# The sums of a recurrence with the heads' halves exchanged, and its value products moved into a second job

## The chip, the cores and the metric

The kernel runs on one core of a Trainium2 chip. The metric is the time of one execution on the device in microseconds (us). Three executions of the kernel before took 1149.68 to 1152.16 us, with a median of 1150.76.

## The reference

One layer of a diffusion backbone is computed for 128 context tokens and 512 latent tokens, 640 in all. It has two branches, a recurrence in both directions (RWKV-7, 8 heads of 64) and a neighbourhood attention, whose outputs are gated, merged and followed by a feed-forward part. The change lies in the recurrence:

```python
def _wkv_step(s, inp):
    r, w, k, v, a, b = inp
    sa = jnp.einsum("bhvk,bhk->bhv", s, a)
    s = s * w[:, :, None, :] + sa[..., None] * b[:, :, None, :] + v[..., None] * k[:, :, None, :]
    return s, jnp.einsum("bhvk,bhk->bhv", s, r)
...
    s_f, y_f = _wkv_scan(s0[:, 0], rh, ..., False)
    s_b, y_b = _wkv_scan(s0[:, 1], rh, ..., True)
    y = y_f + y_b
    mean = jnp.mean(y, axis=-1, keepdims=True)
    var = jnp.mean(jnp.square(y - mean), axis=-1, keepdims=True)
```

Each head carries a state s of 64x64 from token to token. Every token reads the state with r, and the outputs of the two directions are summed to y and normalised per head.

## The kernel before, in words

The recurrence is not run token by token. The 640 tokens form 10 blocks of 64 ("slots": 0 to 7 latent, 8 and 9 context), and with two directions each pair of heads has 20 "lines", one for each block and direction. Within a line everything is a product of 64x64 matrices; between the lines of a sequence runs the state. The four pairs of heads (ct 0 to 3) are worked through one after the other. The two heads of a pair lie on the partitions 0 to 63 and 64 to 127 (`hrows[0]`, `hrows[1]`), so that a product of 64x64 uses one quarter of TensorE's array: which rows of the array says where its input lies, which columns says where its output goes. A product with `hrows[h]` for both is on a diagonal quarter, one that goes from `hrows[h]` to `hrows[1 - h]` on the other two.

For each pair there are four stages:

- `main` makes the matrices N of all lines (`n_job`).
- `inv` inverts a triangular matrix for each line in 30 steps on VectorE (DVE). At three of the steps, named by a table, it lets TensorE (PE) do a group of lines: first lines 8 to 11, then 0 to 7, then 12 to 19. For a group, `v_job` turns v by products with an identity (`idh(h)`) and copies it to ZV on ScalarE (ACT); `t_job` turns B and K and copies them to TG; `g_job` makes the products that are masked on DVE to AG and TG. The value products of lines 10 to 19 (`flip`) already stand in `g_job`. At the end the inverse is put together as Rt (L1345 to L1364).
- `carry`, the sweep, takes the eight steps s in turn, with two lines each (four in steps 0 and 1, where the context blocks go along). A step has three phases. In the first, PE makes AG·ZV (L1400), which ACT copies to x0 (L1403); then PE adds the outputs of the step before to Y (`ysum`, L1380), begins the new state `pn` by products of the identity with ZV (L1415), and adds R·ZV to Y (L1421). In the second, PE multiplies Rt with x0 (L1430) and ACT copies the result to ZV (L1436). In the third, PE finishes `pn` (L1443) and DVE scales it to the ZV of the next line (L1455). Between the phases the generator yields, and a plan written out by hand puts in a number of matmuls of a projection that does not depend on the recurrence ("fillers", L223). Y is two accumulators, one for the slots 0 to 7, copied to y at the sweep's end (L1462), and one for the slots 8 and 9, copied at step 2 (L1406).
- `out` normalises y with statistics from matmuls (L1472) and passes it on.

The accumulators (`wps()`) are taken in turn from six buffers. On every engine the instructions stand in the order in which the program issues them.

The identity products and the Y products, as they stand before:

```python
                    for g, (sl, d, l) in todo:
                        for h in range(2):
                            if sl != 8:
                                own = hrows[h]
                                pe.matmul(pn[own, g * 64:g * 64 + 64], idh(h), ZV[own, l, h, :],
                                          start=once(pn, h), stop=False)
```

Of the kernel before, what the change touches and what calls it, by code (L numbers as in the profile page):

```python
# [108 lines left out]
def V(ap, dims, off=0):  # L109

    return bass.AP(ap.tensor, ap.offset + off, [list(ap.ap[0])] + [list(d) for d in dims])
# [3 lines left out]
def body(ctx: ExitStack, tc: tile.TileContext, xs, xp, cols, consts, w_ada, b_row, w_rw, w_qkv,  # L115
# [3 lines left out]
    pe, act, dve, pool, sp = nc.tensor, nc.scalar, nc.vector, nc.gpsimd, nc.sync  # L119
# [40 lines left out]
    def idh(h):  # L160
        return K[64 * h:64 * h + 64, KO["ident"] + 64 * h:KO["ident"] + 64 * h + 64]
# [935 lines left out]
    with ExitStack() as s3:  # L1097
# [12 lines left out]
        v = vp0  # L1110
# [10 lines left out]
        def wps():  # L1121
            return pp.tile([P, 512], F32, tag="w", bufs=6, name=nm("w"))
# [53 lines left out]
        def sq(t, n):  # L1176
            return V(t[:, :], [[64, n], [1, 64]])
# [18 lines left out]
        def g_job(S, l0, l1):  # L1196
            n = l1 - l0

            f0 = max(l0, 10)
            pv = wps() if l1 > f0 else None  # L1200
            pg, pr = wps(), (wps(), wps())
            for l in range(l0, l1):
                if l >= f0:
                    flip(pv, l, f0)
                o_ = slice(64 * (l - l0), 64 * (l - l0) + 64)
                b, k = (S.BK[l // 10][:, l % 10, i, :] for i in range(2))
                for h in range(2):
                    pe.matmul(pg[hrows[1 - h], o_], k[hrows[h], :], AG[hrows[h], l, h, :], start=True, stop=True)
                for x, i in ((b, 0), (k, 1)):
                    for h in range(2):  # L1210
                        pe.matmul(pr[h][hrows[h ^ i], o_], x[hrows[h], :], R_[hrows[h], l, :],
                                  start=True, stop=True)
            ls = slice(l0, l1)
            if l1 > f0:
                v_out(pv, f0, l1 - f0)

            def masks():
                for h in range(2):
                    oth = hrows[1 - h]
                    dve.tensor_tensor(out=AG[oth, ls, h, :], in0=sq(pg, n)[oth],  # L1220
                                      in1=V(K[oth, :], [[0, n], [1, 64]], KO["strict"]), op=ALU.mult)
                for h in range(2):
                    dve.tensor_tensor(out=TG[:, ls, h, 1, :], in0=sq(pr[h], n),
                                      in1=V(K[:, :], [[0, n], [1, 64]], KO["incl"]), op=ALU.mult)

            return masks

        def v_job(S, l0, l1):

            if l0 > 9:  # L1230
                return
            n = min(l1, 10) - l0
            pv = wps()
            for l in range(l0, l0 + n):
                for h in range(2):
                    pe.matmul(pv[hrows[1 - h], 64 * (l - l0):64 * (l - l0) + 64], v[hrows[h], 64 * l:64 * l + 64],
                              idh(h), start=True, stop=True)
            v_out(pv, l0, n)

        def v_out(pv, l0, n):  # L1240
            for h in range(2):
                act.copy(ZV[hrows[1 - h], l0:l0 + n, h, :], sq(pv, n)[hrows[1 - h]])

        def flip(pv, l, l0):

# [122 lines left out]
        def carry(ct, S, last):  # L1368
# [4 lines left out]
            Y = [wps(), wps()]  # L1373
            begun, back = [], []

            def ysum(items):

                for (sl, d, l) in items:
                    for h in range(2):
                        pe.matmul(V(Y[sl // 8][hrows[h], :], *ycol(sl, d)), ZV[:, l, h, :], TG[:, l, h, 1, :],  # L1380
                                  start=once(Y[sl // 8], h), stop=sl in (7, 9) and d == 1)

            def once(t, h):
# [4 lines left out]
            def ycol(sl, d):  # L1388

                n = 8 if sl < 8 else 2  # L1390
                return ([[-1, 64]], 64 * (n - sl % 8) - 1) if d else ([[1, 64]], 64 * (sl % 8))

            for s in range(8):
# [9 lines left out]
                act.copy(x0[:, :ng, :], V(px[:, :], [[64, ng], [1, 64]]))  # L1403
                ysum(back)
                if s == 2:
                    act.copy(y[:, 512:640], Y[1][:, 0:128])  # L1406
                todo = [(g, i) for g, i in enumerate(items) if i[0] != 7]
                if todo:

                    pn = wps()  # L1410
                    for g, (sl, d, l) in todo:
                        for h in range(2):
                            if sl != 8:
                                own = hrows[h]
                                pe.matmul(pn[own, g * 64:g * 64 + 64], idh(h), ZV[own, l, h, :],  # L1415
                                          start=once(pn, h), stop=False)
                for (sl, d, l) in items:
                    for h in range(2):
                        own = hrows[h]
                        if sl != 8:  # L1420
                            pe.matmul(V(Y[sl // 8][own, :], *ycol(sl, d)), ZV[own, l, h, :], R_[own, l, :],  # L1421
                                      start=once(Y[sl // 8], h), stop=False)
                if s == 7 and not PRM["lh"][ct]:
                    last()
                yield
# [33 lines left out]
                if s == 7:  # L1459
                    ysum(items)  # L1460
                yield
            act.copy(y[:, 0:512], Y[0][:, 0:512])  # L1462

        def out(ct, S):

# [694 lines left out]
```

## Time and profile before

| | before |
|---|---|
| median of three runs | 1150.76 us (1149.68 to 1152.16) |
| the profiled execution | 1150.25 us |
| its span in the trace | 1148.5 us |
| PE matmul busy | 1115.5 us, 97% of the span |
| PE weight loads busy | 989.1 us, 86% |
| DVE busy | 778.9 us, 68% |
| ACT busy | 535.4 us, 47% |
| GpSimd (POOL) busy | 195.3 us, 17% |
| recurrence in the span | from about 256 to 629 us |

The span is what the trace covers, and 1.75 us of the profiled execution lie around it. Busy times of PE are those of its matmuls, whose ends are modelled; the loads of weights (PEld) run beside them. A float32 product of 64x64 stands in the trace as two records. In a row of the trace, "out<-in" names the tiles, "128x64" the partitions and elements, "x8" the records grouped, and the bracket tells how long the engine had been idle and which instruction it had waited for.

### The profile page before, as it was taken

What the parts mean: (1) busy time and instruction counts of PE and PEld (TensorE: products, weight loads), DVE (VectorE), ACT (ScalarE), POOL (GpSimd) and SP (SyncE); (2) the same over time, 40 slices, a digit from 0 to 9 for tenths busy, and PEclk for the clock granted to TensorE, in tenths of its full rate; (3) what the DMA queues carried; (4) which work ended last, traced back from release to release, by engine and by line L of the source; (5) the groups of instructions that cost most, each with busy time, mean ns of one, the idle gap of its engine ahead of it and who ended that gap; (6) DMA issues with size and microseconds to landing.
All of it is one profiled execution on the core that took longest, in us unless ns stands there. A gap on an engine that the chain in (4) does not pass through costs nothing.

```text
span 1148.5 us, 26859 instructions
## 1 busy us (share of the span) xinstructions
PE 1115.5 (97%) x11160; PEld 989.1 (86%) x11160; DVE 778.9 (68%) x1641; ACT 535.4 (47%) x1052; POOL 195.3 (17%) x262
## 2 busy tenths in 40 slices
PE   6999999999999999999999999999999999999998
PEld 4688878789888988888898788999899989998997
DVE  4565465769558847945786846897478747874775
ACT  4444566655465665556343525654134413441340
POOL 1163244320101202120100521110101010101000
PEclk9999999999999999999999999999999999999999
DMA  9752677654433533343733971223212321232122
GB/s 341 264 119 83 205 277 230 203 150 122 109 75 86 142 91 93 107 108 86 268 108 105 269 213 67 92 93 94 90 56 92 95 90 55 92 96 89 55 92 93
DMA packets 60482, 149.16 MB, mean 130 GB/s; under 512 B 7460, under 2 KB 22436, under 8 KB 60360
## 3 DMA queue, kind: packets, MB, share of 16 engines
q1 hardware_dynamic: 54888, 131.16, 34.8%
q0 software_dynamic: 4032, 14.68, 6.5%
q8 instruction: 88, 1.44, 0.5%
q10 hardware_dynamic: 1440, 1.59, 0.5%
q14 instruction: 34, 0.28, 0.1%
HBM read 118.41 MB, written 14.32 MB: 116 GB/s over the span
## 4 chain that ended last, share of the span: by engine, by line
PE 74%; DVE 10%; issue 8%; ACT 3%; DMA 3%; POOL 1%; SPq 0%; DVEq 0%; ACTq 0%; POOLq 0%
PE acc L311 24%; PE f L1863 21%; PE fl L223 9%; PE mm L223 5%; DVE RL L1321 1%; DVE pr L1317 1%; PE lg L959 1%; PE po L1006 1%; PE pt L988 1%; PE psa L1044 1%; DVE Rt L1353 1%; DMA wa<-in_w_ada_dram 1%; DMA f<-in_w_ada_dram 1%; PE w L1400 1%; PE w L1430 1%
## 5 line engine op out<-in xcount | busy, mean ns | idle before, releaser
L1863 PE MATMUL f<-t,whi 128*128 128x320 f32 x640 | 141.7, 309 | 0.2
L311 PE MATMUL acc<-whi,u 128*128 128x512 f32 (+1 forms) x448 | 136.0, 385 | 0.0
L1863 PE MATMUL f<-b,whi 128*128 128x320 f32 x608 | 135.0, 310 | 0.4 <-DVE b L212 0.4
L223 PE MATMUL fl<-h,whi 128*128 128x320 f32 x672 | 120.8, 320 | 0.0
L1863 PEld LDWEIGHTS f<-t,whi 128*128 128x128 f32 x640 | 106.8, 188 | 0.8 <-issue 0.4
L223 PEld LDWEIGHTS fl<-h,whi 128*128 128x128 f32 x672 | 101.1, 188 | 4.8
L192 ACT CAST whi<-wst 128x1024 fp32r<-128x1024 f32 (+1 forms) x77 | 79.4, 1034 | 54.5 <-PE acc L311 41.8
L1863 PEld LDWEIGHTS f<-b,whi 128*128 128x128 f32 x608 | 101.7, 188 | 1.1 <-issue 0.6
L1863 PE MATMUL f<-t,wlo 128*128 128x320 f32 x320 | 98.9, 309 | 0.0
L311 PEld LDWEIGHTS acc<-whi,u 128*128 128x128 f32 x448 | 83.5, 188 | 16.7
L1863 PE MATMUL f<-b,wlo 128*128 128x320 f32 x304 | 94.0, 309 | 0.0
L1916 ACT CAST whi<-ws 128x1024 fp32r<-128x1024 f32 x40 | 42.1, 1053 | 104.4 <-PE f L1863 45.6
L311 PE MATMUL acc<-wlo,u 128*128 128x512 f32 (+1 forms) x224 | 86.3, 385 | 0.0
L1930 POOL TENSOR_TENSOR ws<-wst 128x512 f32<-128x512 f32 x20 | 29.0, 1449 | 334.9 <-DVE wlo L1919 226.3
L195 DVE TENSOR_TENSOR wlo<-wst,whi 128x1024 fp32r<-128x1024 f32 (+2 forms) x57 | 60.9, 1077 | 30.7 <-ACT whi L192 30.0
L311 PE MATMUL acc<-whi,h 128*128 128x512 f32 x240 | 78.9, 403 | 0.7 <-DVE h L436 0.7
L1731 DVE SCALAR_TENSOR_TENSOR tt<-acc,G 128x512 f32<-128x512 f32 (+1 forms) x51 | 34.7, 680 | 59.3 <-PE acc L311 45.4
L223 PE MATMUL fl<-h,wlo 128*128 128x320 f32 x336 | 63.0, 318 | 0.0
L1916 ACT CAST whi<-wst 128x1024 fp32r<-128x1024 f32 (+1 forms) x48 | 41.4, 870 | 42.3 <-PE acc L311 25.1
L1863 PEld LDWEIGHTS f<-t,wlo 128*128 128x128 f32 x320 | 60.1, 188 | 0.0
L1919 DVE TENSOR_TENSOR wlo<-ws,whi 128x1024 fp32r<-128x1024 f32 x40 | 55.5, 1387 | 5.4 <-ACT whi L1916 5.4
L1455 DVE TENSOR_TENSOR ZV<-w,Dt 64x128 f32<-64x128 f32 x64 | 18.5, 289 | 58.7 <-PE w L1443 57.6
(342 smaller groups left out, 2536.3 us busy)
## 6 DMA issues: line engine op xcount, KB each, us to landing
wst<-in_w_dram SPq DMA_DIRECT2D x66, 512.0 KB
wst<-in_w_rw_dram SPq DMA_DIRECT2D x31, 512.0 KB
wlo<-wst POOLq DMA_DIRECT2D x28, 512.0 KB, 4.9
wa<-in_w_ada_dram SPq DMA_DIRECT2D x24, 512.0 KB
f<-in_w_ada_dram SPq DMA_DIRECT2D x16, 512.0 KB
wst<-in_w_qkv_dram SPq DMA_DIRECT2D x12, 512.0 KB
o<-o_d SPq DMA_DIRECT2D x14, 320.0 KB
x<-in_xs_dram SPq DMA_DIRECT2D x8, 512.0 KB
```

Of the source, the lines that this page charges most:

```text
L192: act.copy(hi[:, :n], st[:, :n])
L195: dve.tensor_tensor(out=lo[:, a:b], in0=st[:, a:b], in1=hi[:, a:b].bitcast(F32), op=ALU.subtract)
L223: pe.matmul(ps[:, :t1 - t0], w[:, a:a + 128], x[:, k0 + kt, t0:t1], start=n == 0, stop=n == 3 * nk - 1)
L311: pe.matmul(pss[i][:, a:b], lhs(x, kt, ts_), w[:, cs_], start=ki == 0 and n == 0, stop=ki == last and n == 2)
L959: pe.matmul(psl[:, hd, o_:o_ + n], qT[ft][rows, qs], x[rows, :], start=True, stop=True)
L988: pe.transpose(pst[:, c * 128:(c + 1) * 128], L[:, c * 128:(c + 1) * 128], ident)
L1455: dve.tensor_tensor(out=V(ZV[own, l + 1, h, :], [[128 * dl, 2], [1, 64]]), in0=V(pn[own, :], [[64, 2], [1, 64]], 64 * g), in1=V(Dt[own, 0, ...
L1731: dve.scalar_tensor_tensor(out=tt, in0=ps[:, a:b], scalar=c, in1=G[:, g, sl], op0=ALU.mult, op1=ALU.mult)
L1863: pe.matmul(ps[:, :H2], w_[:, c_], x_[:, kt, :], start=first and kt + n == 0, stop=last and kt == 3 and n == 2, skip_group_check=more)
L1916: act.copy(r[0][:, :width], src())
L1919: dve.tensor_tensor(out=r[1][:, :width], in0=src(), in1=r[0][:, :width].bitcast(F32), op=ALU.subtract)
L1930: eng_x(PRM["se"][i - 1]).tensor_tensor(out=o_, in0=x, in1=y, op=op)
```

## The change

There are two parts.

In the sweep, the outputs are summed with the halves of the two heads exchanged: the output of the head on partitions 0 to 63 is now accumulated on partitions 64 to 127 of Y, and the other way round, in `ysum` and in the R·ZV products alike. These products then lie on the two quarters that the identity products leave free. The two loops, identity products and R·ZV products, become one that issues both for each line in turn. When Y is copied to y, two copies of 64 partitions each exchange the halves back (`y_out`), in the place of one copy of 128 partitions.

In the inverse, the value products of lines 0 to 7 are no longer a job ahead of `t_job`. They stand in `g_job` line by line (`turn`), on the diagonal quarters, and `v_out` exchanges the halves when it copies them to ZV. That copy now comes after the TG copies. Lines 8 and 9 keep their own job, with `turn` and exchanged copies as well.

```diff
@@ -1197,9 +1197,11 @@
             n = l1 - l0
 
             f0 = max(l0, 10)
-            pv = wps() if l1 > f0 else None
+            pv = wps()
             pg, pr = wps(), (wps(), wps())
             for l in range(l0, l1):
+                if l0 == 0:
+                    turn(pv, l, 0)
                 if l >= f0:
                     flip(pv, l, f0)
                 o_ = slice(64 * (l - l0), 64 * (l - l0) + 64)
@@ -1211,7 +1213,9 @@
                         pe.matmul(pr[h][hrows[h ^ i], o_], x[hrows[h], :], R_[hrows[h], l, :],
                                   start=True, stop=True)
             ls = slice(l0, l1)
-            if l1 > f0:
+            if l0 == 0:
+                v_out(pv, 0, 8, 0)
+            else:
                 v_out(pv, f0, l1 - f0)
 
             def masks():
@@ -1227,19 +1231,21 @@
 
         def v_job(S, l0, l1):
 
-            if l0 > 9:
+            if l0 != 8:
                 return
-            n = min(l1, 10) - l0
             pv = wps()
-            for l in range(l0, l0 + n):
-                for h in range(2):
-                    pe.matmul(pv[hrows[1 - h], 64 * (l - l0):64 * (l - l0) + 64], v[hrows[h], 64 * l:64 * l + 64],
-                              idh(h), start=True, stop=True)
-            v_out(pv, l0, n)
-
-        def v_out(pv, l0, n):
+            for l in range(8, 10):
+                turn(pv, l, 8)
+            v_out(pv, 8, 2, 0)
+
+        def turn(pv, l, l0):
             for h in range(2):
-                act.copy(ZV[hrows[1 - h], l0:l0 + n, h, :], sq(pv, n)[hrows[1 - h]])
+                pe.matmul(pv[hrows[h], 64 * (l - l0):64 * (l - l0) + 64], v[hrows[h], 64 * l:64 * l + 64],
+                          idh(h), start=True, stop=True)
+
+        def v_out(pv, l0, n, x=1):
+            for h in range(2):
+                act.copy(ZV[hrows[1 - h], l0:l0 + n, h, :], sq(pv, n)[hrows[h ^ x]])
 
         def flip(pv, l, l0):
 
@@ -1373,11 +1379,17 @@
             Y = [wps(), wps()]
             begun, back = [], []
 
+            def y_out(i):
+
+                a, n = ((0, 512), (512, 128))[i]
+                for h in range(2):
+                    act.copy(y[hrows[h], a:a + n], Y[i][hrows[1 - h], 0:n])
+
             def ysum(items):
 
                 for (sl, d, l) in items:
                     for h in range(2):
-                        pe.matmul(V(Y[sl // 8][hrows[h], :], *ycol(sl, d)), ZV[:, l, h, :], TG[:, l, h, 1, :],
+                        pe.matmul(V(Y[sl // 8][hrows[1 - h], :], *ycol(sl, d)), ZV[:, l, h, :], TG[:, l, h, 1, :],
                                   start=once(Y[sl // 8], h), stop=sl in (7, 9) and d == 1)
 
             def once(t, h):
@@ -1403,23 +1415,22 @@
                 act.copy(x0[:, :ng, :], V(px[:, :], [[64, ng], [1, 64]]))
                 ysum(back)
                 if s == 2:
-                    act.copy(y[:, 512:640], Y[1][:, 0:128])
+                    y_out(1)
                 todo = [(g, i) for g, i in enumerate(items) if i[0] != 7]
                 if todo:
-
                     pn = wps()
-                    for g, (sl, d, l) in todo:
+                for g, (sl, d, l) in enumerate(items):
+                    if sl == 8:
+                        continue
+                    if sl != 7:
                         for h in range(2):
-                            if sl != 8:
-                                own = hrows[h]
-                                pe.matmul(pn[own, g * 64:g * 64 + 64], idh(h), ZV[own, l, h, :],
-                                          start=once(pn, h), stop=False)
-                for (sl, d, l) in items:
+                            own = hrows[h]
+                            pe.matmul(pn[own, g * 64:g * 64 + 64], idh(h), ZV[own, l, h, :],
+                                      start=once(pn, h), stop=False)
                     for h in range(2):
                         own = hrows[h]
-                        if sl != 8:
-                            pe.matmul(V(Y[sl // 8][own, :], *ycol(sl, d)), ZV[own, l, h, :], R_[own, l, :],
-                                      start=once(Y[sl // 8], h), stop=False)
+                        pe.matmul(V(Y[sl // 8][hrows[1 - h], :], *ycol(sl, d)), ZV[own, l, h, :], R_[own, l, :],
+                                  start=once(Y[sl // 8], h), stop=False)
                 if s == 7 and not PRM["lh"][ct]:
                     last()
                 yield
@@ -1459,7 +1470,7 @@
                 if s == 7:
                     ysum(items)
                 yield
-            act.copy(y[:, 0:512], Y[0][:, 0:512])
+            y_out(0)
 
         def out(ct, S):
 
```

The order of the instructions on PE, in step 6 of the first pair's sweep (before; w_3807 is Y, w_4266 is `pn`, and K holds the identity):

```order
L1400 MATMUL w_4255<-ZV,AG 64x64 x4
L1380 MATMUL w_3807<-TG,ZV 64x64 x4
L1415 MATMUL w_4266<-ZV,K 64x64 x4
L1421 MATMUL w_3807<-R__2901,ZV 64x64 x4
L1430 MATMUL w_4275<-x_682_4260,Rt 64x64 x4
```

The same place in the changed kernel, where `pn` is w_4267 and the lines are numbered anew (L1428 is L1415 before, L1432 is L1421):

```order
L1412 MATMUL w_4256<-ZV,AG 64x64 x4
L1392 MATMUL w_3807<-TG,ZV 64x64 x4
L1428 MATMUL w_4267<-ZV,K 64x64 x2
L1432 MATMUL w_3807<-R__2901,ZV 64x64 x2
L1428 MATMUL w_4267<-ZV,K 64x64 x2
L1432 MATMUL w_3807<-R__2901,ZV 64x64 x2
L1441 MATMUL w_4276<-x_682_4261,Rt 64x64 x4
```

The eight products of the identity and of R now stand in pairs by turns, between the same neighbours.

The second place is the group of lines 0 to 7 on PE, in the first pair's inverse. Before, where w_3193 takes the v products and w_3212 and w_3213 those of `t_job`, its start reads:

```order
L1236 MATMUL w_3193<-K,vp_627 64x64 x16
L1259 MATMUL w_3212<-K,f_518_2684 64x64
L1259 MATMUL w_3213<-K,f_518_2684 64x64
L1259 MATMUL w_3212<-K,f_518_2684 64x64
L1259 MATMUL w_3213<-K,f_518_2684 64x64
```

In the changed kernel the group starts with `t_job`, and a line of `g_job` behind it reads (w_3229 takes the v products, w_3230 those for AG, w_3231 and w_3232 those for TG):

```order
L1243 MATMUL w_3229<-K,vp_627 64x64 x2
L1210 MATMUL w_3230<-AG,f_518_2684 64x64 x2
L1213 MATMUL w_3231<-R__2901,f_518_2684 64x64
L1213 MATMUL w_3232<-R__2901,f_518_2684 64x64
L1213 MATMUL w_3231<-R__2901,f_518_2684 64x64
L1213 MATMUL w_3232<-R__2901,f_518_2684 64x64
```

The sixteen v products have moved from the head of the group into its last job, two to each line.

On ACT the same group's copies, before:

```order
L551 ACTIVATE kt__626<-U_2911,D 128x512
L1242 COPY ZV<-w_3193 64x8x64 x2
L1262 COPY TG<-w_3212 128x8x64
L1262 COPY TG<-w_3213 128x8x64
L190 ACTIVATE wlo_3301<-wst_3034 128x1024
```

And in the changed kernel:

```order
L551 ACTIVATE kt__626<-U_2911,D 128x512
L1268 COPY TG<-w_3193 128x8x64
L1268 COPY TG<-w_3194 128x8x64
L1248 COPY ZV<-w_3229 64x8x64 x2
L190 ACTIVATE wlo_3301<-wst_3034 128x1024
```

The copies of v have gone behind those of TG. Beside this, ACT has eight instructions more in all, the second halves of the y copies, and DVE, POOL and SP have theirs in the order of before.

## The prediction

> **What bounds the kernel now.** I read the page first, then a table of the windows of the recurrence, then the timeline of one step, then the waits inside it. On the page PE is busy nearly all the time:
>
> ```profile
> PE 1115.5 (97%) x11160; PEld 989.1 (86%) x11160; DVE 778.9 (68%) x1641; ACT 535.4 (47%) x1052; POOL 195.3 (17%) x262
> ```
>
> The change touches only the recurrence. Its four head pairs follow each other, each with an inverse and then a sweep; the table gives them in turn (stretch, length, busy time of PE, PEld, DVE, ACT and POOL, granted clock, DMA share, GB/s):
>
> ```profile
> 256.00:298.00 42.00, 41.88 (x864) 39.63 (x863) 40.48 (x144) 21.16 (x45) 5.01 (x13) 1.00 0.48 122
> 298.00:342.00 44.00, 42.05 (x558) 36.54 (x557) 17.92 (x37) 27.96 (x71) 4.99 (x8) 0.96 0.31 78
> 342.00:397.00 55.00, 53.13 (x1088) 49.41 (x1086) 50.27 (x158) 29.03 (x56) 11.25 (x21) 1.00 0.46 121
> 397.00:438.00 41.00, 40.71 (x557) 36.12 (x557) 20.52 (x38) 28.44 (x72) 7.39 (x11) 1.00 0.29 74
> 438.00:493.00 55.00, 51.96 (x1076) 47.86 (x1074) 47.28 (x155) 28.43 (x56) 11.32 (x19) 1.00 0.42 110
> 493.00:536.00 43.00, 42.44 (x568) 37.72 (x568) 18.12 (x36) 28.43 (x72) 5.28 (x10) 1.00 0.33 89
> 536.00:598.00 62.00, 58.28 (x1106) 53.93 (x1106) 49.90 (x156) 27.85 (x57) 6.04 (x11) 1.00 0.56 187
> 598.00:629.00 31.00, 30.55 (x506) 25.83 (x501) 19.88 (x48) 10.81 (x35) 0.00 (x0) 1.00 0.37 110
> ```
>
> The sweeps (second, fourth, sixth and eighth row) are PE's: 96 to 99% busy, with DVE at half or less in the first three. In the inverses DVE is nearly as full as PE (40.48 of 42.00 in the first). So PE time taken from a sweep should shorten it unless another engine's answer is awaited; PE time taken from an inverse shortens it only where DVE is not what ends it. One step of a sweep, number 6 of the first pair:
>
> ```profile
> 332.10 0.45 PE L1400 MATMUL w<-ZV,AG 128*64 128x64 f32 x8
> 332.38 0.40 PE L1380 MATMUL w<-TG,ZV 128*64 128x64 f32 x8
> 332.60 0.27 ACT L1403 COPY x<-w 128x128 f32<-128x128 f32 x1 [2.65 <-PE w L1400]
> 332.72 0.45 PE L1415 MATMUL w<-ZV,K 64*64 64x64 f32 x8
> 333.00 0.40 PE L1421 MATMUL w<-R__2901,ZV 64*64 64x64 f32 x8
> 333.18 0.32 PEld L1430 LDWEIGHTS w<-x,Rt 64*64 64x64 f32 x8
> ```
>
> L1400 makes the product that ACT copies to x0; L1430 needs x0. The old outputs (L1380), the identity products (L1415) and the Y products (L1421) fill the time of that copy. It ends at 332.87 and the weights of L1430 start at 333.18: 0.31 us later. That slack is what a shorter L1415 and L1421 can use up.
>
> **The unit of PE time.** Two records of the trace are one 64x64 product. Two products on diagonally opposite quarters of the array, or four on all quarters, should cost the same time; these rows show it. The first two are stretches (length, PE busy and records), the others starts of lines inside the job for masked products, without and with its two flips of v:
>
> ```profile
> 263.68:265.50 1.82, 1.82 (x96) 1.00 0.00 0
> 276.85:277.83 0.98, 0.98 (x65) 1.00 0.98 228
> 265.60 0.22 PE L1208 MATMUL w<-AG,f 64*64 64x64 f32 x1
> 265.83 0.22 PE L1208 MATMUL w<-AG,f 64*64 64x64 f32 x1
> 277.83 0.23 PE L1248 MATMUL w<-ZV,J 64*64 64x64 f32 x2
> 278.06 0.23 PE L1248 MATMUL w<-ZV,J 64*64 64x64 f32 x2
> ```
>
> The second stretch is the t job alone: 32 products on four quarters, 0.98/8 = 0.12 us a slot of four. The first is v and t: 1.82 - 0.98 = 0.84 for the v job, whose 16 products use two quarters only, so 0.84/8 = 0.105 a slot of two. Inside the masked job a line of six products takes 265.83 - 265.60 = 0.23, and a line with two more on the free quarters 278.06 - 277.83 = 0.23 too: two products added on free quarters cost nothing. I take 0.117 us a slot, half of a line of 0.235.
>
> **The change, part by part.** Carry: identity and Y products took two slots each per step (0.47 in the rows above, from L1415's start to the end of L1421's slots) and now share two. Steps 0 and 2 to 6 save two slots each, step 1 with two extra items four, step 7, with no identity products, none: 16 slots a sweep, 64 in all, 64 x 0.117 = 7.5 us of PE time. The v products of lines 0 to 7 go into the masked job on its free quarters: eight slots a pair, 32 in all, 3.7 us. The bound from above is 11.2 us.
>
> Not all comes through. Step 0 saves nothing: Rt, the last product of the inverse, is late in three pairs, as here, and in the last pair x0 is:
>
> ```profile
> 297.83 0.19 PEld L1430 LDWEIGHTS w<-x,Rt 64*64 64x64 f32 x4 [0.26 <-DVE Rt L1364]
> 396.09 0.96 PE L1430 MATMUL w<-x,Rt 64*64 64x64 f32 x14 [0.79 <-DVE Rt L1364]
> ```
>
> Steps 1 and 2 have the slack, here in the last pair:
>
> ```profile
> 602.23 0.37 ACT L1403 COPY x<-w 128x256 f32<-128x256 f32 x1 [0.95 <-PE w L1400]
> 603.52 0.55 PEld L1430 LDWEIGHTS w<-x,Rt 64*64 64x64 f32 x16
> 607.15 0.27 ACT L1403 COPY x<-w 128x128 f32<-128x128 f32 x1 [0.86 <-PE w L1400]
> 607.91 0.32 PEld L1430 LDWEIGHTS w<-x,Rt 64*64 64x64 f32 x8
> ```
>
> Slack is 603.52 - 602.60 = 0.92 against 0.47 saved, and 0.49 against 0.235: 0.70 a sweep, 2.8 in all. Of the 16 steps 3 to 6, eight have the slack, from step 4 of the first pair (0.31, as in step 6 above) to step 6 of the last, first two rows below; in seven the copy comes last, since ACT casts weights or evaluates another function first, as in the three rows after; in one 0.11 is left.
>
> ```profile
> 622.89 0.27 ACT L1403 COPY x<-w 128x128 f32<-128x128 f32 x1 [1.27 <-PE w L1400]
> 623.41 0.32 PEld L1430 LDWEIGHTS w<-x,Rt 64*64 64x64 f32 x8
> 418.85 1.05 ACT L192 CAST whi<-wst 128x1024 fp32r<-128x1024 f32 x1
> 419.79 0.28 ACT L1403 COPY x<-w 128x128 f32<-128x128 f32 x1
> 420.12 0.31 PEld L1430 LDWEIGHTS w<-x,Rt 64*64 64x64 f32 x8 [0.43 <-ACT x L1403]
> ```
>
> Slack of 0.25 less the 0.05 from the copy's end to the load (420.07 to 420.12) gives 0.20 to 0.235 in each of the eight: 1.8, and 0.1 for the one. Steps where ACT's queue decides also take back part of what an earlier step of their sweep saved, since that queue does not move; I put 0.45 for two such places, bounded by 0 and by all that steps 1 to 6 of the first three pairs save, about 3.2. Carry: 2.8 + 1.8 + 0.1 - 0.45 = about 4.2, of which the last pair, with no ACT queue in the way, has 0.70 + 4 x 0.205 = 1.5.
>
> The v products. In the first two pairs the wait for Rt above ends the inverse whatever PE does before: nothing. In the third, DVE waits for PE and ACT in its masks and afterwards (first two rows); in the fourth PE itself waits, for the copies behind L1479, and the v copy is the first of them:
>
> ```profile
> 459.68 1.39 DVE L1220 TENSOR_TENSOR AG<-w,K 64x512 f32<-64x512 f32 x2 [0.18 <-PE w L1208]
> 477.36 0.35 DVE L552 SCALAR_TENSOR_TENSOR kt__626<-U,C,kt__626 128x128 f32<-128x128 f32 x1 [0.59 <-ACT kt__626 L551]
> 561.72 1.17 ACT L1242 COPY ZV<-w 64x512 f32<-64x512 f32 x2
> 562.95 0.25 PEld L1211 LDWEIGHTS w<-R__2901,f 64*64 64x64 f32 x9 [0.49 <-ACT ZV L1242]
> ```
>
> I take 0.6 for the third (between 0.18 and 0.77, the sum of both idles; nearer the upper because both follow PE's order) and 0.6 for the fourth: with the v copy last, the accumulator that L1211 waits for comes free after one t copy and not after the v copies. Together 1.2, between 0 and 3.7.
>
> ACT's part. y now leaves in two half copies. A 64x128 copy takes half of the 0.55 below and a 64x512 one half of the 1.17 above, no less than the whole copy of 0.59 below; so 0.27 more at step 2 and 0.58 more at the end of each sweep. Behind the first stands the copy of ZV, which idles 0.58 before it; behind the second the next pair's work, or in the last pair the norm, for which ACT was idle 0.90 before.
>
> ```profile
> 314.28 0.55 ACT L1436 COPY ZV<-w 64x128 f32<-64x128 f32 x2 [0.58 <-PE w L1430]
> 628.85 0.59 ACT L1462 COPY out<-w 128x512 f32<-128x512 f32 x1 [0.90 <-PE w L1380]
> 304.85:308.26 3.41, 3.41 (x68) 0.50 0.45 155
> ```
>
> I cost it at nothing; with no cover left it is 4 x 0.85 = 3.4. DVE, POOL and SP keep their order, and no DMA is moved. PE idles of the kind "issue" in dense code stay as they are.
>
> The sum: 4.2 + 1.2 = 5.4. The profiled execution took 1150.25 (span 1148.5 and 1.75 around it) and the median of the runs is 1150.76, 0.5 above it; so 1144.85 for the profiled one, and 1145.4 as the median. What a measurement of this kernel can tell from no change is about 0.2%, 2.3 us.
>
> **A rule that speaks against it.** The step's rows give four quarters 16 records in two slots of 0.117, 15 ns a record, and the t job 0.98/65 = 15 ns, where two quarters alone take 0.105/4 = 26 to 29 ns. The Trainium skill, page "TensorE: Matmul & The Clock Gate", section "Wait — 56ns, not 53.3ns?", says that matmuls never start closer than about 25 ns apart, however small. By that rule four quarters could not be filled: 16 records would need 0.40 us in a step and not 0.235, an estimate by that page, and the carry would save 0.07 a step in place of 0.235. The trace disagrees with it, with 65 records in 0.98 us in this very kernel, so the measurement decides.
>
> **The rivals.**
> - *All of PE's saving comes through* (0.10). For it: the sweeps' 96 to 99% on PE. Against: the late copies above. 11.2 less one or two lost: about 10, 1140.8.
> - *Absorbed* (0.17). ACT's queue and DVE's order set the first three pairs, and what PE saves there turns into the waits of 0.43 and 0.79 shown. Only the last pair's 1.5 + 0.6 = 2.1 is left: 1148.7.
> - *The change doesn't do what it says* (0.08): in the carry the quarters do not overlap, since its products use the K identity, ZV and R as weights by turns, or the two accumulators hinder each other. Then a step stays at 0.47 and the sum near 0: 1150.8. Against it: the t job alternates two accumulators as well. The rule above is this rival's, with a result of its own: 16 slots a sweep at 0.035 in place of 0.117 give 64 x 0.035 = 2.2, little of it beyond the steps with slack, 1149 to 1150.
> - *Slower, by the clock* (0.12). The last row above is a stretch at half clock in the first sweep, 3.41 us long: it cost 1.7. It is the only one in the recurrence (0.96 in its row of the table and 1.00 in all others). PE will now idle up to 0.9 us longer for Rt at an inverse's end and longer for x0 in late steps. If such idles call the stretches up, one or two eat 1.7 to 3.4 of the gain, and from five on, (5.4 + 2.3)/1.7 = 4.5, the kernel is slower: 5 x 1.7 - 5.4 = 3.1, 1153.9. Against it: the longest of these waits, 0.79 at 396.09, is followed by no such stretch.
>
> **How the numbers follow.** The forecast has 0.53, and its own range is 1143 to 1148. The range reaches down to the first rival, 1140.5, and up to the third, 1150.9; what it leaves out is the slower rival's 0.12 and the far end of the first, 0.03. Faster by over 0.2%, under 1148.5: the forecast, the first rival and a third of the second's spread, 0.53 + 0.10 + 0.06 = 0.69. Within 0.2%: the rest of the second, 0.11, and 0.07 of the third, 0.18. Slower: 0.12 and 0.01 of the third.
>
> **What would show it.** In the changed profile, identity and Y products of a step should take 0.24 together where L1415 and L1421 take 0.47, and in the steps with slack L1430's weights should start 0.05 to 0.1 after x0's end; in the late steps the wait for x0 should grow from 0.43 to about 0.66. The v and t jobs of lines 0 to 7 should take 0.98 and not 1.82, with the masked job's line still at 0.235. The waits for Rt should grow by up to 0.84. The sweeps should be shorter by 0.8 to 1.5 us each. The forecast is wrong if a step's products still take over 0.4, if sweeps save under 0.5 each, if a second stretch at half clock shows, or if ACT's half copies of y stand ahead of a copy that PE waits for.

## The result, and the profile after

The changed kernel took 1147.05 us (median of 22 runs, 1144.37 to 1151.26), and the kernel before, run beside it, 1150.36 (22 runs). The ratio is 0.9967, with a 95% interval of 0.9958 to 0.9976: 2.8 to 4.8 us faster, where 5.4 was forecast. The profiled execution took 1147.09 with a span of 1145.3, against 1150.25 and 1148.5 before. In the changed kernel L1412 is L1400 before, L1415 the copy to x0 (L1403), L1428 and L1432 the identity and R products (L1415, L1421), L1441 the products with Rt (L1430), L1213 and L1210 those of the masked job (L1211, L1208).

The page's busy times:

```profile
PE 1108.9 (97%) x11160; PEld 980.9 (86%) x11160; DVE 777.6 (68%) x1641; ACT 538.4 (47%) x1060; POOL 195.3 (17%) x262
```

The four sweeps, each from its first to its last load for AG·ZV; first the changed kernel, then the kernel before (stretch, length, PE busy and records, granted clock, DMA share, GB/s):

```profile
297.31:335.01 37.70, 36.34 (x548) 1.00 0.30 79
391.54:430.28 38.74, 37.07 (x542) 0.96 0.34 92
489.11:526.05 36.94, 35.96 (x544) 1.00 0.43 114
595.47:623.17 27.70, 27.17 (x485) 1.00 0.42 124
```

```profile
295.81:336.97 41.16, 39.98 (x548) 0.96 0.28 73
393.81:431.95 38.14, 36.98 (x543) 1.00 0.35 96
491.01:528.79 37.78, 37.22 (x543) 1.00 0.43 111
597.01:626.21 29.20, 28.75 (x485) 1.00 0.39 117
```

The third and fourth sweep can be compared as they stand: 0.84 and 1.50 us shorter (forecast 0.87 and 1.5). The first two can't: a stretch at half clock lies in the first sweep before and in the second after.

Step 6 of the first pair, on the timeline of the changed kernel:

```profile
330.38 0.45 PE L1412 MATMUL w<-ZV,AG 128*64 128x64 f32 x8
330.66 0.40 PE L1392 MATMUL w<-TG,ZV 128*64 128x64 f32 x8
330.88 0.27 ACT L1415 COPY x<-w 128x128 f32<-128x128 f32 x1 [2.67 <-PE w L1412]
331.00 0.27 PE L1428 MATMUL w<-ZV,K 64*64 64x64 f32 x2
331.01 0.27 PE L1432 MATMUL w<-R__2901,ZV 64*64 64x64 f32 x2
331.22 0.32 PEld L1441 LDWEIGHTS w<-x,Rt 64*64 64x64 f32 x8
```

From the first identity product to the load of L1441 it is 331.22 - 331.00 = 0.22 us, where it was 333.18 - 332.72 = 0.46 before: two slots in place of four. The load for L1441 now comes 0.07 after the end of the copy (331.15), where it came 0.31 after. What holds PE next is seen where the copy is late, and in the summed waits of PE's loads from 290 to 640 us (total, times, longest):

```profile
418.35 0.28 ACT L1415 COPY x<-w 128x128 f32<-128x128 f32 x1
418.69 0.31 PEld L1441 LDWEIGHTS w<-x,Rt 64*64 64x64 f32 x8 [0.65 <-ACT x L1415]
...
PEld w L1441 <- ACT x L1415: 3.2, 11, 0.6
```

The step that waited 0.43 waits 0.65, and all waits for x0 have grown to 3.2 us in 11 steps; before they were 0.9 in 3. So 2.3 of the 7.5 us of PE time saved in the sweeps were waited away in late steps.

### The profile page after: what moved, and what is told of

Its sections match the earlier page's. It is cut to its first block, busy times and chain, and to the rows that moved or that the text cites. A ratio compares the mean times of both kernels' runs of the same rounds, so it can differ in the third digit from the quotient of the medians.

```text
span 1145.3 us, 26868 instructions
## 1 busy us (share of the span) xinstructions
PE 1108.9 (97%) x11160; PEld 980.9 (86%) x11160; DVE 777.6 (68%) x1641; ACT 538.4 (47%) x1060; POOL 195.3 (17%) x262
## 3 DMA queue, kind: packets, MB, share of 16 engines
q8 instruction: 88, 1.44, 0.5%
## 4 chain that ended last, share of the span: by engine, by line
PE 73%; DVE 9%; issue 8%; ACT 5%; DMA 4%; POOL 1%; SPq 0%; DVEq 0%; ACTq 0%; POOLq 0%
PE acc L311 24%; PE f L1874 23%; PE fl L223 10%; PE mm L223 4%; DVE RL L1327 1%; DVE pr L1323 1%; DMA o_d<-on 1%; PE lg L959 1%; PE po L1006 1%; PE pt L988 1%; PE psa L1044 1%; DMA wa<-in_w_ada_dram 1%; PE w L1441 1%; DMA o<-o_d 1%; PE w L1412 1%
## 5 line engine op out<-in xcount | busy, mean ns | idle before, releaser
L1874 PEld LDWEIGHTS f<-b,wlo 128*128 128x128 f32 x304 | 57.1, 188 | 0.1
```

The source lines that it names most:

```text
L1874: pe.matmul(ps[:, :H2], w_[:, c_], x_[:, kt, :], start=first and kt + n == 0, stop=last and kt == 3 and n == 2, skip_group_check=more)
```

## The experiments

Each kernel ran beside the kernel before on one chip. "Loss at half clock" below is (1 - mean granted clock) x span, averaged over a kernel's runs; a stretch of 3.4 us at half clock loses 1.7. Over all 223 runs with a recorded clock, each kernel with a mean of its own, the span grows by 0.50 us (0.41 to 0.58) per us of it, and "at equal clock" is the difference to before with that taken out.

| kernel | runs | ratio to before, interval | loss at half clock | at equal clock, us |
|---|---|---|---|---|
| before (beside and again) | 96 | | 3.3 | 0 |
| the change, again | 12 | 0.9977 (0.9960 to 0.9993) | 6.3 | -4.0 ± 0.9 |
| sweep's half alone | 8 | 0.9962 (0.9948 to 0.9977) | 3.4 | -4.0 ± 1.0 |
| v part alone | 12 | 0.9998 (0.9987 to 1.0010) | 4.0 | 0.0 ± 0.9 |
| loops apart | 12 | 0.9981 (0.9970 to 0.9993) | 5.1 | -3.1 ± 0.9 |
| y copies twice | 12 | 0.9979 (0.9968 to 0.9989) | 6.4 | -4.4 ± 0.9 |
| short inverse, before | 12 | 0.9987 (0.9973 to 1.0002) | 3.7 | -1.6 ± 0.9 |
| short inverse, changed | 6 | 0.9940 (0.9920 to 0.9959) | 3.8 | -7.0 ± 1.2 |
| other fillers (refill) | 12 | 1.0019 (1.0004 to 1.0033) | 7.1 | +0.5 ± 0.9 |
| fillers in the jobs (spread) | 12 | 1.0009 (0.9995 to 1.0023) | 5.8 | -0.7 ± 0.9 |
| the same on the sweep's half | 7 | 0.9966 (0.9953 to 0.9979) | 4.3 | -4.7 ± 1.1 |

**The two parts.** The sweep's half alone: `g_job`, `v_job` and `v_out` as before.

> The sweep's half of the change alone; the v products stand as before. My theory (the trace of the changed kernel lost 0.5 to 1.5 us in each sweep, and what it won in the inverses was mostly waited away): 2.5 to 4.0 us faster than before, nearly all of the whole change's 3.3. Rival one (the gain is the v products', and the sweep's goes into waits for x0): under 1 us faster. Rival two (the sweep gains more than the whole shows and the v part costs): over 4 us faster. The identity and output products of a step should take two slots, 0.24 us, as in the whole change.

It took 1146.61 beside 1151.36: 2.6 to 6.0 us faster. Its sweeps were 39.49, 37.11, 36.92 and 27.65 us long, that is 1.67 (with a shorter wait for Rt), 1.03, 0.86 and 1.55 less than before. All of the gain is in this half. The ratio gives 4.4 us, more than the whole change's 3.3 and inside rival two, but the interval holds the theory's 2.5 to 4.0 as well, and at equal clock the half and the whole are both at 4.0.

The v part alone: `carry` as before.

> The inverse's half of the change alone: the v products of lines 0 to 7 in the masked job, the sweep as before. My theory: 0.2 to 1.2 us faster, since the first two inverses end on DVE's Rt whatever PE does, and the waits for Rt grow by 0.5 to 0.9. Rival one: 2.5 to 3.7 us faster (all of the 32 slots come through). Rival two: slower by up to 1 us, because the masks' accumulators now wait for the t copies on ACT (0.6 in the changed trace).

It took 1151.53 beside 1151.36, a ratio of 0.9998: between 1.5 us faster and 1.2 slower, so nothing that these runs can tell, and neither the theory nor rival two is ruled out. Its sweeps are as before (third and fourth 37.79 and 29.19). Where the eight slots of a pair went, the job of lines 0 to 7 tells, from its first load to its last, in the profiled executions:

| kernel | pair 1 | pair 2 | pair 3 | pair 4 |
|---|---|---|---|---|
| before | 3.68 | 3.67 | 4.27 | 4.25 |
| before, again | 3.67 | 3.68 | 4.32 | 4.81 |
| sweep's half alone | 3.68 | 3.68 | 4.10 | 4.25 |
| changed | 2.82 | 2.76 | 3.85 | 3.87 |
| changed, again | 3.60 | 2.76 | 4.14 | 4.07 |
| v part alone | 2.87 | 2.76 | 4.14 | 4.22 |
| loops apart | 3.35 | 2.76 | 4.47 | 4.84 |

(In the fourth pair, "before, again" and "v part alone" lie partly in a stretch at half clock.) In the first two pairs the job lost its 0.9 us (in two runs of the first less), and waits behind it took them, as forecast, though not for Rt alone: in the changed kernel PE waits 0.99 and 0.59 ahead of the products with N (L1351), where it waited 0.19 before, and for Rt in the second pair 1.13 for 0.93. In the third pair the job is only 0.1 us shorter on the mean, and in the fourth, without those two, not shorter on the mean (from 0.4 shorter to 0.6 longer): PE stops inside it. The rows are the ends of these stops in the changed kernel, in the kernel before and with the loops apart, all in the third pair, and what DMA did from 454 to 458 us of the changed kernel, in 40 slices of 0.1 us:

```profile
456.87 0.14 PEld L1213 LDWEIGHTS w<-R__2901,f 64*64 64x64 f32 x3 [0.92 <-issue]
```

```profile
458.83 0.14 PEld L1208 LDWEIGHTS w<-AG,f 64*64 64x64 f32 x2 [0.51 <-issue]
```

```profile
459.41 0.14 PEld L1213 LDWEIGHTS w<-R__2901,f 64*64 64x64 f32 x3 [1.54 <-issue]
```

```profile
DMA  0000005000000000000000000000000000000008
GB/s 0 0 0 0 0 0 164 0 0 0 0 0 0 0 0 0 0 0 0 0 0 0 0 0 0 0 0 0 0 0 0 0 0 0 0 0 0 0 0 164
...
q8 instruction: 2, 0.03, 3.7%
```

The only DMA in this stretch is two packets of the instruction queue, 0.03 MB together. The first starts at 454.7 and by its record takes 0.9 us, to 455.6; PE goes on 1.3 us after that. That is no chance. In the recurrences of all thirteen profiles PE's loads have 86 idles of 0.28 us or more that the trace calls issue. Of these, 57 stand inside a job of small products, and each of the 57, which last up to 2.88 us, ends 1.24 to 1.58 us after an instruction packet has ended; of all loads of the jobs that make N, TG and AG only 5% lie in that interval. The other 29 stand ahead of the first product of a job or a step and end 3.8 to 7.3 us after the last packet. The queue q8 is PE's by its size: 1.44 MB in 88 packets over the span are 65 bytes for each of PE's 22320 matmuls and loads. So PE waits for its program there. The Trainium skill, page "Runtime: NRT & Kernel Launch", section "Instruction fetch mechanics", says that the sequencer refills in 16 KiB blocks while it executes, and that the cost of crossing a block is mostly hidden. The packets' size agrees with it (0.03 MB for two); that it is hidden does not hold here. In such a place the job takes as long as its instructions take to arrive. The v products moved onto free quarters need the same instructions, so in the third pair the stop grew, from 0.46 on the mean with the old v job (0.30 to 0.57) to 1.22 with the new one (0.92 to 1.54), by most of the 0.9 that the array saved.

In the fourth pair something else stands in the way too. The rows are PE's wait inside the job and the work of ACT ahead of it, in the changed kernel:

```profile
559.50 0.92 ACT L1490 ACTIVATE out<-out,C 128x640 f32<-128x640 f32 x1 [5.82 <-DVE out L1489]
560.45 1.07 ACT L1268 COPY TG<-w 128x512 f32<-128x512 f32 x2
561.09 0.14 PEld L1213 LDWEIGHTS w<-R__2901,f 64*64 64x64 f32 x3 [0.61 <-ACT TG L1268]
```

Before, PE waited 0.49 here for the copies of v. Now the copy of TG comes first, but it still stands behind an activation that DVE releases (L1490), and PE, which has no v job to do, waits 0.61 for it.

**Is it the sharing of the quarters?** In the changed kernel the loop over `items` was split in two again:

```diff
-                for g, (sl, d, l) in enumerate(items):
-                    if sl == 8:
-                        continue
-                    if sl != 7:
-                        for h in range(2):
...
+                for g, (sl, d, l) in enumerate(items):
+                    if sl in (7, 8):
+                        continue
+                    for h in range(2):   # identity products
...
+                for g, (sl, d, l) in enumerate(items):
+                    if sl == 8:
+                        continue
+                    for h in range(2):   # R products, exchanged halves
```

> The whole change, but the identity products of a step stand in one loop and the R products, still on the exchanged quarters, in a second one behind it, as before. It tells whether sharing the quarters in time is what saves. My theory: a step's products take four slots again, 0.47 us, and the kernel keeps only the v part: 0 to 1.2 us faster than before. Rival (the exchange as such saves, for example by other accumulator reads, or PE reaches from one loop into the other by itself): 2.5 us faster or more, as the whole change.

I was wrong. It is 0.8 to 3.5 us faster than before, and its third and fourth sweeps, 36.98 and 27.78, are within 0.1 of the changed kernel's. The program issues four identity products of a step and then four R products, as the order shows:

```
L1427 MATMUL w_4015<-ZV,K 64x64 x4
L1434 MATMUL w_3807<-R__2901,ZV 64x64 x4
```

(step 2 of the first pair, in products; each is two records in the trace). The trace has them in turn; these are rows of step 2 in the last pair:

```profile
608.11 0.27 PE L1427 MATMUL w<-ZV,K 64*64 64x64 f32 x2
608.14 0.27 PE L1434 MATMUL w<-R__2901,ZV 64*64 64x64 f32 x2
608.22 0.23 PE L1427 MATMUL w<-ZV,K 64*64 64x64 f32 x2
608.25 0.23 PE L1434 MATMUL w<-R__2901,ZV 64*64 64x64 f32 x2
608.28 0.22 PE L1427 MATMUL w<-ZV,K 64*64 64x64 f32 x2
```

A product on a free quarter starts before earlier products whose quarters are taken. So the exchange of the halves saves by itself; writing the two kinds in turn adds at most 0.1 us a sweep here.

**Does the clock take some of it?** The kernel before and the changed kernel, each once more:

> The kernel before, unchanged, to see how its runs spread and which clock they were granted. Its ratio to before: 1.000 within 0.001. Theory one (the stretches at half clock come at random in both kernels): its mean clock over the runs is the changed kernel's 0.9948, within 0.0010. Theory two (longer idling of PE in the changed kernel calls more of them up and eats part of the gain): its mean clock is 0.9960 or more, that is at least 1.4 us less time lost at half clock than in the changed kernel.

> The changed kernel, unchanged, beside runs of the kernel before whose granted clock is listed too. It tells whether the changed kernel loses more time at half clock. Theory one (the stretches come at random): mean clock within 0.0010 of before's on the same chip, and both the plain and the clock-adjusted difference 3.5 to 5.5 us. Theory two (PE idles longer at the inverses' ends and this calls up stretches at half clock): mean clock at least 0.0015 lower than before's, and the plain difference at least 0.8 us smaller than the adjusted one.

The kernel before came out at 0.9997 (0.9986 to 1.0008), with a mean clock of 0.9970. The changed kernel was 0.8 to 4.6 us faster. Its mean granted clock was 0.9945, and that of the kernel before beside it 0.9966 (29 runs); in its first 22 runs it had been 0.9946. Of the two theories' numbers these are theory two's: (0.9966 - 0.9945) x 1147 = 2.4 us more lost at half clock than before on the same chip, 1.4 stretches, which at 0.50 cost some 1.2 us. Where a stretch lies is known of the profiled executions alone. In the two profiles of the changed kernel these lie in the recurrence (first profile, then the second):

```profile
394.75:398.25 3.50, 3.50 (x31) 0.51 0.15 52
555.00:558.75 3.75, 3.39 (x12) 0.54 1.04 405
```

```profile
302.75:306.25 3.50, 3.50 (x26) 0.51 0.08 16
398.25:402.00 3.75, 3.75 (x29) 0.54 0.14 48
545.00:548.75 3.75, 3.75 (x16) 0.54 0.43 131
```

One near 395 stands in both. It follows the end of the second inverse, where PE now idles 1.13 for Rt (second row; 0.93 before); the first row is the wait ahead of the first products with N in the first inverse, where the v part's gain went there:

```profile
287.77 1.38 PEld L1351 LDWEIGHTS w<-f,Nt 32*32 32x32 f32 x80 [0.99 <-issue]
394.02 0.20 PEld L1441 LDWEIGHTS w<-x,Rt 64*64 64x64 f32 x4 [1.13 <-DVE Rt L1370]
```

What calls them up I can't settle: the sweep's half alone has 3.4 us of loss, the v part alone 4.0, and both together 6. One more number on this stands in the table: in the changed kernel with a short inverse (below), which has no wait for Rt, the loss is 3.8, as in its own base (3.7). That fits theory two, but it rests on six runs.

**Can the waits be filled?** In the plan of the changed kernel (the entries that differ, with most others left out):

```diff
-  first pair:  ... 24.0.0 20.0.0 10.0.0 8.0.0 8.0.0 ...
+  first pair:  ... 24.0.0 25.0.0 10.0.0 13.0.0 8.0.0 ...
-  second pair: ... 24.0.0 20.0.0 10.0.0 ... "10.0 0.0 7.1 ...
+  second pair: ... 24.0.0 23.0.0 10.0.0 ... "17.0 0.0 7.1 ...
```

> The changed kernel with another plan of fillers: ten more before the end of the first pair's inverse (five ahead of L1351, five ahead of L1365) and ten more in the second pair's (three ahead of L1351, seven ahead of the first step). They stand in the waits that the changed trace shows there (0.99, 1.13, 0.59 and 1.13 us) and are missing nowhere else but at the end of the supply. Theory (the v products' saving is turned into these waits, and a wait can be filled): 1.0 to 3.0 us faster than the changed kernel. Rival (ACT or DVE set the pace behind these places too, or the fillers are wanted later): within 0.7 us of the changed kernel.

It failed: at 1153.66 it was 0.5 to 3.8 us slower than the kernel before. In its profile the wait for Rt in the second pair is gone, but every later filler stands elsewhere: the waits for x0 come to 7.7 us (3.2 in the changed kernel), the third sweep starts 3.5 us later than in the changed kernel's profile, and near the end of the supply PE waits 3.4 us at once for a gate made on DVE. Its loss at half clock is as large as the changed kernel's, so that wait for Rt alone does not account for it; since other and longer waits have come in (up to 2.2 us for x0), this does not clear idling as the cause.

**Does DVE hide the v part?** `if 18 <= s <= 23: pass` ahead of DVE's work of a step, in both kernels. Both leave out a part of the inverse, so they do not compute the layer; they only show what the time does:

> The kernel before with DVE's part of the steps 18 to 23 of every inverse left out, so that DVE is done about 5 us earlier and no longer ends the inverse. It is the base for the next run. Faster than before by 1.5 to 4 us (the waits for Rt go), and the waits for Rt gone from its trace.

> The changed kernel with the same steps of DVE left out. Theory (the v part's gain is lost because DVE ends the inverses): against the kernel before with the same steps left out it is 6.5 to 8 us faster, that is 4.4 of the sweeps and 2.5 to 3.4 of the v products. Rival (the v part gains nothing for another reason, such as the masks' accumulators waiting for ACT): 4 to 5 us faster, no more than the sweeps give.

The first came out at 1148.83, a ratio of 0.9987 (0.9973 to 1.0002), and in its profile no wait for Rt is left. Against each other the two differ by 1148.83 - 1143.74 = 5.1 us, 5.4 ± 1.4 at equal clock: between the two expectations, and the interval reaches into both. With DVE out of the way the job of lines 0 to 7 saved 0.64 and 0.92 in the first two pairs (3.04 and 2.76, against 3.68 twice) and lost 0.22 and 0.60 in the others to stops for instructions (4.13 and 4.89 against 3.91 and 4.29), 0.74 in all. So with DVE out of the way the v part gives about 1 us (0.7 by the jobs, 1.4 ± 1.7 by the times, after the sweeps' 4.0, which alone can't be told from nothing); the rest never came.

**Can the stops for instructions be filled?** In the third pair, between `t_job` and `g_job`:

```diff
                     for f in (v_job, t_job):
                         f(S, *jobs[s])
+                    for _ in range({9: 7, 28: 8}.get(s, 0) if ct == 2 else 0):
+                        next(fill, False)
                     masks.append(g_job(S, *jobs[s]))
```

with as many taken from the plan's next entries, and 6 and 5 fillers moved ahead of the first job in the second and third pair.

> The changed kernel with fillers moved to where PE stops inside its dense jobs of small products (the idles of 0.9 to 1.9 us that the trace calls issue, each of which ends 1.2 to 1.6 us after a packet of the instruction queue has landed). In the third pair, 7 fillers go between the t job and the masked job of lines 0 to 7 and 8 between those of lines 12 to 19; 6 and 5 go ahead of the first job of the second and third pair. Each is taken from the next fillers behind, so their number is unchanged. Theory (these stops are waits for instructions, and useful work that needs few instructions fills them): the stops of 1.0 to 1.3 and 1.4 to 1.8 in the third pair's jobs fall under 0.4, and the kernel is 1 to 2.5 us faster than the changed one, less two changes of shape of 0.26 each. Rival one (the stop is tied to a place in the code, not to time): it stays, 0 to 0.5 slower. Rival two (the inverse's end waits for DVE anyway): the stops go, and the time is within 0.5.

> The same fillers moved, on the kernel with the sweep's half of the change alone (v products as before). There the stop in the job of lines 0 to 7 was only 0.4, so less is to be had: theory, 0.5 to 1.5 us faster than the sweep's half alone, and so no faster than the run before by more than its interval. Rival (the v part costs by its longer stops): this one is the fastest of all, by 1 us or more over the spread changed kernel.

The stops of the third pair fell to 0.34 and 0.28 (from 0.92 and 1.71), here with L1198 and L1201 for L1210 and L1213:

```profile
455.57 0.13 PEld L1198 LDWEIGHTS w<-AG,f 64*64 64x64 f32 x2 [0.34 <-issue]
470.22 0.13 PEld L1201 LDWEIGHTS w<-R__2901,f 64*64 64x64 f32 x1 [0.28 <-issue]
...
478.04 0.71 PEld L1341 LDWEIGHTS w<-f,Nt 32*32 32x32 f32 x39 [0.91 <-DVE f L1328]
488.61 0.19 PEld L1431 LDWEIGHTS w<-x,Rt 64*64 64x64 f32 x4 [0.65 <-DVE Rt L1360]
...
PEld acc L299 <- DMA wlo<-wst: 3.0, 1, 3.0
```

So useful work fills such a stop. But it brought no time. In the third pair PE now waits for DVE (third and fourth row), 0.91 ahead of the products with N, where the changed kernel waits 0.19, and 0.65 for Rt, where it does not wait: rival two holds there. From the end of the second sweep to the end of the third it takes 95.5 us, in the changed kernel 95.8. In this profile the stage behind the recurrence begins at 644.42 and in the changed kernel's at 647.60, but two stretches at half clock lie in the latter's recurrence and none here; in the profile with the copies of y issued twice (below), which has the plan of the changed kernel and no such stretch there either, it begins at 644.04:

```profile
644.04 0.34 PEld L311 LDWEIGHTS acc<-whi,m 128*128 128x128 f32 x2
```

Behind it PE waits 3.0 us for a weight tile whose transfer is late (last row above), where the changed kernel waits 0.6. The kernel took 1151.45, no faster than before and slower than the changed kernel (1.0009 against 0.9967 and 0.9977). On the sweep's half alone the same moves gave 1146.80, as without them, and so less than the theory's 0.5 to 1.5 us; its rival came true, that this is the fastest of all and over 1 us faster than the spread changed kernel: with the moved fillers the v part costs 4.0 ± 1.3 us at equal clock. Where these are lost is not shown beyond the waits above. No version tried here beats the sweep's half by more than the intervals.

**ACT's copies of y.** `for h in (0, 1, 0, 1)` in `y_out`:

> The changed kernel with its half copies of y issued twice over, which adds 0.55 us of ACT work at step 2 and 1.17 at the end of each sweep, more than the change itself adds (0.28 and 0.58). Theory (ACT's part is covered): within 0.6 us of the changed kernel. Rival (the copies stand in the way of work that PE waits for): 2 to 6 us slower than the changed kernel, and the change itself then pays 1 to 3 us for them.

It took 1148.41 beside 1150.73, a ratio of 0.9979, as the changed kernel's 0.9977 when run again. The copies are covered. In the changed kernel's last sweep the pair of half copies takes 1.17 us, and the next ACT work stands right behind it without being waited for:

```profile
625.81 1.17 ACT L1386 COPY out<-w 64x512 f32<-64x512 f32 x2 [0.91 <-PE w L1392]
627.01 0.83 ACT L192 CAST whi<-wst 128x768 fp32r<-128x768 f32 x1
```

## Why the prediction was right or wrong

- *The sweeps, 4.2 us: right.* The sweep's half alone gives 4.0 ± 1.0 at equal clock, and the sweeps forecast at 0.87 and 1.5 lost 0.84 and 1.50. The steps with slack came down to 0.07 after the copy, and the wait of 0.43 in a late step grew to 0.65, as worked out (0.66).
- *The unit of 0.117 us a slot, also for four quarters: right in the sweep.* 16 records in 0.22 us are 14 ns a record. The floor of about 25 ns that the Trainium skill gives ("TensorE: Matmul & The Clock Gate", "Wait — 56ns, not 53.3ns?") would need 0.40, an estimate by that page; this trace disagrees.
- *What saves in the sweep: only half understood.* The prediction has the products share two slots and does not say whether it is the exchange or the order in turn that brings it; the expectation of the run with loops apart took the order to be needed. The exchanged halves are enough.
- *The v products, 1.2 us: wrong, about 0.* The failed step is the sentence that the idles of the kind "issue" in dense code stay as they are. They are waits for instructions: in the third pair the one in the job of lines 0 to 7 grew from 0.46 to 1.22 on the mean, and in the fourth such stops appeared in some runs (1.11 with the loops apart). The 0.6 of the third pair, from DVE's idle behind PE, was also not there to be had: with the stops filled, PE waited for DVE (0.91 and 0.65). The 0.6 of the fourth was to come from a shorter wait for ACT behind L1479; that wait grew from 0.49 to 0.61, since the activation ahead of the copies did not move. In the first two pairs the reason given, that the inverse ends on DVE, held; with DVE's steps cut short the v part gives at most about 1 us.
- *The slower rival, half-clock stretches: it happened, in part.* With 1.4 more of them a run than before the changed kernel lost about 1.2 us; the prediction had put "one or two" at 1.7 to 3.4 and five as the point of deciding. One of its own signs of being wrong, a second stretch at half clock, came: two lie in the recurrence of the first profile. The cause, longer idling, is not shown: one such idle was filled and the loss stayed, but other idles came in.
- *ACT's part at nothing: right,* even with the copies doubled.
- *The sum.* 4.0 for the sweeps, 0.0 for the v products and 1.2 lost to the clock give 2.8; the runs gave 2.8 to 4.8 at first and 0.8 to 4.6 when run again, and the first 22 runs at equal clock 5.2 ± 0.7, if the clock of the runs of before beside them was as in the later ones (it was not recorded). Within that spread the sum can't be made sharper. The forecast's range held because it was wide enough for a term that came to nothing.

## What to carry to other kernels

Price a saving on the array in dense runs of small products only after looking for idles that no semaphore ends: if each follows an instruction packet, the run is as long as its instructions, and only fewer instructions or work with few instructions per us can fill it. Filling it pays only if no other engine ends the stage right behind, as DVE did here. Putting two independent products on different quarters of the array is worth it even if they are issued in separate loops close together. And in a program packed this tightly, a saving in the middle moves to the next late arrival (a copy, a transposed matrix, a weight tile): find what is late next before counting it.

## What the runs showed of the hardware

- PE starts small products out of the order of issue when their quarters are free: R products 0.03 us after the first identity products, although six more records of those stood ahead of them in the program.
- PE stops for its program: 57 of 57 stops inside jobs of small products that the trace calls issue end 1.24 to 1.58 us after an instruction packet has ended, and the longest was 2.88 us.
- Runs of one kernel spread by up to 10 us here (1142.46 to 1152.73 for the changed one); about half of what a run loses at half clock by its records comes through to its time (0.50 us per us).
